# Moving work off the critical places of a transformer block on one TensorE: decays, modulation fillers, last head, residual loads

## The chip, the cores and the metric

The kernel runs on one core of a Trainium2 chip. A core has a matrix engine (TensorE, PE in the profile, with its weight loads as PEld), a vector engine (VectorE, DVE), a scalar engine (ScalarE, ACT), GpSimd (POOL), and queues that issue transfers (SyncE, SP). Each engine works through its own instructions in order and waits on semaphores for the others. The metric is the device time of one execution in microseconds; several runs are made and the median is given.

## What is computed

One layer of a generator over 512 latent tokens with 256 context tokens, width 2048, all in float32. The reference, cut to what matters here:

```python
mod = c_act @ w_mod + b_mod                       # six vectors of 2048: sh1, sc1, gt1, sh2, sc2, gt2
h  = rmsnorm(x, g_norm1) * (1 + sc1) + sh1        # and hc, the same for the context
z  = h @ w_in                                     # q, k, v, gates and decays of all heads
# 4 bidirectional GLA heads (gated linear attention), each decay a cumulative sum in the exponent
# 4 bidirectional mLSTM heads (matrix memory, running-max stabiliser)
y  = concat(rmsnorm(gla_o) * silu(gla_gate), sigmoid(ml_ogate) * rmsnorm(ml_h))
x  = x + gt1 * (y @ w_out)
h2 = rmsnorm(x, g_norm2) * (1 + sc2) + sh2
u_gate, u_val = split(h2 @ w_up)
x  = x + gt2 * ((silu(conv3x3(u_gate) + conv_b) * u_val) @ w_down)
out = rmsnorm(x, g_final)
```

`gt1`, `sh2`, `sc2` and `gt2` are four of the six modulation vectors. Each is a product of one vector with a 2048 x 2048 part of `w_mod`, so it costs much loading and little arithmetic. `gt1` is needed at the residual behind w_out, `sh2` and `sc2` for `h2`, `gt2` only at the residual behind w_down.

## The kernel before

All activations are held transposed: features on the 128 partitions, the 512 tokens along the free dimension. A product in float32 is made of three products (`mm3`): each operand is split into a high part, a rounded copy made by ScalarE, and a low part, the difference made by VectorE, and high x high, high x low and low x high are added up in PSUM. `load_split` brings one 512 KB piece of weights through SP's queue into a buffer of the pool `wraw` (four buffers), splits it into `hi` and `lo` (two buffers each), and hands both to the matmuls. A unit is eight such pieces (kp 0 to 7), each with 24 matmuls of 128x512 for four PSUM banks. So an engine that makes `hi` or `lo` late stops TensorE, and a `raw` buffer that is held too long delays the next load.

The stages, in order: the projection of heads 0 and 1; then for every further head its projection woven with the attention work of the head before (`weave`: a generator of stages says by its `yield`s how much projection, in estimated microseconds of TensorE, goes between two pieces of attention work). Heads 0 to 3 are GLA, heads 4 to 7 mLSTM. The last mLSTM head has no projection to be woven with and gets the first of four gate units. Then come gate units 1 to 3, the splitting of `yT`, four units of w_out with the residual `x2`, the second norm (`token_rstd`, `h2`), and the MLP: an `up_gate` unit, its 3x3 convolution on VectorE (eight multiply-adds per 128 features, `cv`), an `up_val` unit, and from time to time the blocks of w_down.

A GLA head works on levels. For each level `gla` makes a tile `ex`: two subtractions on VectorE, two exponentials on ScalarE, a multiplication with q and k, and then the matmuls `sl`. `ex` has two buffers. In the mLSTM head the blocks of tokens are called j; each makes `po`, a normaliser `dn` and the output `ob` on VectorE, and ends with `yield 1.4`.

The four late modulation vectors are made by fillers: small functions in a list. `load_split` pops `rate` of them per load (with a running `credit`). A chunk filler (`mod_chunk`) loads 512 KB of `w_mod` into a `wraw` buffer (`raw_m`); VectorE multiplies one half by a column and adds it up, ScalarE scales the other half, and POOL adds that up. The last of eight chunks adds the two sums on POOL (L259). An end filler (`mod_end`) makes four small matmuls (`mc`, L266), which are kept in program order among each other, and VectorE adds the bias (`mod`). Between chunks and end are entries that do nothing, as a lag. Regions 2, 3 and 4 make 132 entries, popped in the projections of heads 4 to 7 from kp 3 on, in the gate units and in w_out; region 5 makes 40, popped in the MLP behind 20 entries that do nothing.

A scheduler orders the instructions of each engine by priority and estimated readiness. TensorE's work keeps program order up to the end of the heads; work under `high_priority` goes first.

Of the kernel before, what the change touches and what calls it, by code (L numbers as in the profile page):

```python
# [26 lines left out]
H = 4  # L27
# [42 lines left out]
def block_kernel(ctx: ExitStack, tc: tile.TileContext, a: dict, out: bass.AP):  # L70
# [8 lines left out]
    def sub(o, x, y):  # L79
        V.tensor_tensor(out=o, in0=x, in1=y, op=ALU.subtract)  # L80
# [33 lines left out]
    csil = keep.tile([P, 128], F32, name="csil")[:, 0:KT]  # L114
    modc = {n: keep.tile([P, KT], F32, name=f"mod{n}") for n in (2, 3, 4, 5)}
    wraw = pool(ctx, "wraw", 4)
    whi = pool(ctx, "whi", 2)
    wlo = pool(ctx, "wlo", 2)
    actp = pool(ctx, "actp")
# [122 lines left out]
    def mod_chunk(region, n, kp, parts):  # L242

        name = f"m{region}_{n}_{kp}"
        raw = wraw.tile([P, 2, T], F32, name=f"raw_{name}", tag="raw")
        nc.sync.dma_start(raw, a["w_mod2"][region - 2, n, kp])
        if kp == 0:
            parts += [sum_tile(i, name) for i in range(2)]
        dv, po = parts
        ce, co = (csil[:, 2 * kp + i : 2 * kp + i + 1] for i in range(2))  # L250
        if kp == 0:
            V.tensor_scalar(out=dv, in0=raw[:, 0, :], scalar1=ce, scalar2=None, op0=ALU.mult)
            S.activation(po, raw[:, 1, :], AF.Copy, scale=co)
        else:
            V.scalar_tensor_tensor(out=dv, in0=raw[:, 0, :], scalar=ce, in1=dv, op0=ALU.mult, op1=ALU.add)  # L255
            S.activation(raw[:, 1, :], raw[:, 1, :], AF.Copy, scale=co)  # L256
            G.tensor_tensor(out=po, in0=po, in1=raw[:, 1, :], op=ALU.add)  # L257
        if kp == KP - 1:
            G.tensor_tensor(out=po, in0=po, in1=dv, op=ALU.add)  # L259
# [47 lines left out]
    def project_steps(h, banks):  # L307

        for kp in range(KP):
            rate[0] = 2 if h >= H and kp >= 3 else 0  # L310
            wh, wl = load_split(a["w_heads"][h, kp], f"h{h}_{kp}")
            for g in range(6):
                project_chunk(kp, wh, wl, banks[g], g)
                yield (1.36, 1.36, 1.44, 1.44, 1.04, 1.04)[g]
# [319 lines left out]
    def crossed(ex, b, fwd):  # L634
# [3 lines left out]
        at, step = (b, T - b) if fwd else (0, T + b)  # L638
        return bass.AP(ex.tensor, ex.offset + at, [ex.ap[0], [2 * b, n], [step, 2], [1, b]])

    def gla(h, pair, qk, v, kn, vn, yT, prep, fill, after, pending):
        bt, b2, kd, ends = (prep[n] for n in ("bt", "b2", "kd", "ends"))

# [8 lines left out]
                               op0=ALU.mult, op1=ALU.mult)  # L652
        yield fill
        for lv, b in enumerate(LEVELS + [P, 2 * P]):
            ex = wk2.tile([P, 2, T], F32, name=f"ex{h}_{lv}", tag="ex")
            n = T // (2 * b)
            if b < P:
                sf = bt[0].rearrange("p (n a b) -> p n a b", a=2, b=b)
                sb = bt[1].rearrange("p (n a b) -> p n a b", a=2, b=b)
                rf = sf[:, :, 0, b - 1 : b].unsqueeze(2).to_broadcast([P, n, 2, b])  # L660
                rb = sb[:, :, 1, 0:1].unsqueeze(2).to_broadcast([P, n, 2, b])
                sub(crossed(ex, b, True), sf[:, :, ::-1, :], rf)
                sub(crossed(ex, b, False), sb, rb)
                S.activation(ex[:, 0, :], ex[:, 0, :], AF.Exp, scale=DECAY)
                S.activation(ex[:, 1, :], ex[:, 1, :], AF.Exp, scale=-DECAY)
            else:
                for i in range(n):
                    e = 2 * i if b == P else 1
                    for s in range(2):
                        for d in range(2):  # L670

                            at = 2 * b * i + (b if s == d else 0)
                            S.activation(ex[:, s, at : at + b], b2[d][:, at : at + b], AF.Exp,
                                         scale=-DECAY if s else DECAY, bias=ends[:, s, d, e : e + 1])
            if pair:
                mul(ex, ex, pair[0])
            else:
                for i in range(2):
                    mul(ex[:, i, :], ex[:, i, :], qk[i])
            if b <= P:  # L680
                ps = psb(f"sl{h}_{lv}", (P, TJ, P))
                for i in range(TJ):
                    j = i if b < P else i ^ 1
                    mm(ps[:, i, :], ex[:, 1, P * i : P * i + P], ex[:, 0, P * j : P * j + P], start=True, stop=True)
                if b < P:
                    V.copy_predicated(scd, msk[:, lv, :].unsqueeze(1).to_broadcast([P, TJ, P]), ps)
                else:
                    S.copy(sc1, ps)
            else:
                for half in range(2):  # L690
                    ps = psb(f"sl{h}_{lv}_{half}", (P, 2, 2 * P))
                    for ii in range(2):
                        i = 2 * half + ii
                        j0 = 2 * P * (1 - half)
                        mm(ps[:, ii, :], ex[:, 1, P * i : P * i + P], ex[:, 0, j0 : j0 + 2 * P],
                           start=True, stop=True)
                    S.copy(sc2[half], ps)
            if lv == 0:
                pending()
            yield fill  # L700
            if lv in (2, 3, 4, 5, 6, 8):
                next(after, None)
            if lv == 1:

                for j in range(CJ):
                    mul(kd[:, :, j], kd[:, :, j], kn[j].unsqueeze(1).to_broadcast([P, 2, DK]))
                ps = psb(f"cst{h}", (P, 2, DV))
                for d in range(2):
                    for j in range(CJ):
                        mm(ps[:, d, :], kd[:, d, j, :], vn[j][:, 0:DV], start=(j == 0), stop=(j == CJ - 1))  # L710
                S.copy(s0[:, :, 0:DV], ps)
                qi = wtile(f"qi{h}", "qi", 2, T)
                for d in range(2):
                    S.activation(qi[:, d, :], b2[d], AF.Exp, scale=DECAY)
                mul(qi, qi, qk[0].unsqueeze(1).to_broadcast([P, 2, T]))
                yield 1
# [80 lines left out]
    def mlstm(h, _, qk, v, kn, vn, yT):  # L797
# [51 lines left out]
        for j in range(TJ):  # L849
# [16 lines left out]
                    V.scalar_tensor_tensor(out=ob[:, j, :], in0=po[:, 0:DV], scalar=dn, in1=ob[:, j, :],  # L866
                                           op0=ALU.mult, op1=ALU.add)
            S.activation(junk, ob[:, j, :], AF.Square, accum_out=ssq[:, j : j + 1])
            yield 1.4
        yield 5.6  # L870
        finish(h, ob, ssq, yT)

# [5 lines left out]
    def first_stages(tiles):  # L878

        yield from small_rows()  # L880
        prep = gla_prep(0, preps[0])
        for need in (0, 1.4, 0, 3, 1, 0):
            next(prep)
            yield need
        end = yield from gla(0, *tiles, yT, preps[0], 2.2, gla_prep(1, preps[1]), lambda: None)
        q, k, v0, v1, *c = early_sums
        tiles = ([], (q, k), [v[:, b, :] for v in (v0, v1) for b in range(2)],
                 [e[:, 0:DK] for e in c], [e[:, DK:] for e in c])
        end = yield from gla(1, *tiles, yT, preps[1], 2.2, gla_prep(2, preps[2]), end)
        yield 4  # L890
        end()

    def stages(h, tiles):

        yield 2.7
        if h >= H:
            yield from mlstm(h, *tiles, yT)
        elif h + 1 < H:
            end = yield from gla(h, *tiles, yT, preps[h], 4, gla_prep(h + 1, preps[h + 1]), lambda: None)
            yield 5  # L900
            end()
        else:
            end = yield from gla(h, *tiles, yT, preps[h], 2.6, iter(()), lambda: None)
            yield 5
            end()
            yield from ml_gates()

    tiles = evict(0, first)
    for h in range(1, 2 * H):
# [1 line left out]
            accs = [acc(f"a{h + 1}_{g}", BANKS[g]) for g in range(6)]  # L911
            steps = project_steps(h + 1, accs)
        else:
            rate[0] = 1.5
            accs = [acc(f"ga0_{i}") for i in range(4)]
            steps = unit_steps(a["w_gates"][0], "ga0", *hx, accs)
        weave(first_stages(tiles) if h == 1 else stages(h, tiles), steps)
# [9 lines left out]
    st_3 = ExitStack()  # L927
    gp = pool(st_3, "gp", 2)
    rp = pool(st_3, "rp")
    rate[0] = 1.5  # L930
    for g in range(4):
        if g:
            accs = unit(a["w_gates"][g], f"ga{g}", *hx)
        for i in range(4):
# [5 lines left out]

    tc.keep_in_program_order(S.preload_act_table_set("natural_log_exp_and_others"))

    yh, yl, x2 = [], [], []
    for k in range(KT):
        yh.append(acttile(k, "h", f"yTh{k}"))
        yl.append(acttile(k, "l", f"yTl{k}"))
        split(yh[k], yl[k], yT[k])
        x2.append(ytile(k, f"x2_{k}"))
        nc.sync.dma_start(x2[k], a["xT"][k])
    def residual(k, ps, gate, sl=slice(0, T)):  # L950
        xx = x2[k][:, sl]
        V.scalar_tensor_tensor(out=xx, in0=ps, scalar=gate[:, k : k + 1], in1=xx, op0=ALU.mult, op1=ALU.add)
# [28 lines left out]
    sums2 = []  # L981
    for n in range(4):
        accs = unit(a["w_out"][n], f"wo{n}", yh, yl)
        with tc.high_priority():
            for i in range(4):
                residual(4 * n + i, accs[i], modc[2])
# [18 lines left out]

    fp = pool(ctx, "fp")
    tp = pool(ctx, "tp", 4)
    cwt = fp.tile([P, NF, 9], F32, name="cwt")
    cbt = fp.tile([P, 152], F32, name="cbt")[:, 0:NF]
    nc.sync.dma_start(cwt, a["conv_w"])  # L1010
# [7 lines left out]
    def sum_tile(i, name):  # L1018
        return fp.tile([P, T], F32, name=f"sum{i}_{name}", tag=f"g{'hl'[i]}10")

    rate[0] = 1.5
    fillers += [lambda: None] * 20
    mod_fillers((5,), 2)

    def up_gate(q):
# [167 lines left out]
```

## Time and profile before

| | before |
|---|---|
| median of 3 runs | 2600.23 us (2597.21 to 2606.91) |
| profiled execution | 2597.59 us |
| its span | 2595.9 us |
| TensorE busy | 2541.1 us, 98% of the span |
| VectorE busy | 1356.0 us, 52% |
| mean granted TensorE clock | 0.994 |
| `raw_m` loads (modulation) | 192 of 512 KB, 4.4 us to landing |

The engines' rows give busy time, its share of the span and the number of instructions. In a list of waits, each row has the waiting engine, tile and line, then the engine, tile and line that released it, the total time, the number of times and the longest. In a timeline a row has the start, the duration, engine, line, operation and tiles, and in brackets the idle time before it with what ended that. In a row of windows the engines' busy times stand in the order PE, PEld, DVE, ACT, POOL (only POOL, or none, where one engine was asked for), then the granted clock of TensorE, the share of the DMA engines and GB/s.

### The profile page before, as it was taken

How to read it: one execution, taken by the hardware profiler on the slowest of the kernel's cores; microseconds unless marked ns; L12 is line 12 of the kernel's file. 1: busy time of each engine (PE TensorE's matmuls, PEld its weight loads, DVE VectorE, ACT ScalarE, POOL GpSimd, SP SyncE). 2: the span in 40 equal slices, each digit the busy share in tenths (PEclk: the TensorE clock that was granted, in tenths of full speed). 3: DMA queues.
4: the chain of work that ended last, by engine and by line, in shares of the span. 5: the costliest groups of instructions: out<-in, count | busy, mean ns of one | idle time of the engine just before them, and what ended most of it. 6: DMA issues, size and time to landing. Idle time of an engine off the chain costs nothing.

```text
span 2595.9 us, 31962 instructions
## 1 busy us (share of the span) xinstructions
PE 2541.1 (98%) x12882; PEld 2134.8 (82%) x12882; DVE 1356.0 (52%) x1969; ACT 873.9 (34%) x1289; POOL 228.1 (9%) x183
## 2 busy tenths in 40 slices
PE   6999999999999999999999999999999999999998
PEld 4887888888897888878878888888888888888887
DVE  6557765543334465458576336532653365336544
ACT  4225543332333343334433123312331233123332
POOL 0000001021222323210321000000000000000001
PEclk9999999999999999989999999999999999999999
DMA  9741112121333666532654222322232223222333
GB/s 383 269 155 34 33 41 90 66 98 66 122 122 126 214 226 216 199 114 101 211 178 141 96 97 97 98 97 98 98 98 98 97 98 97 96 96 87 100 97 102
DMA packets 96349, 321.39 MB, mean 124 GB/s; under 512 B 10884, under 2 KB 15304, under 8 KB 96200
## 3 DMA queue, kind: packets, MB, share of 16 engines
q1 hardware_dynamic: 96200, 319.34, 35.8%
q8 instruction: 101, 1.65, 0.3%
q14 instruction: 48, 0.39, 0.0%
HBM read 315.10 MB, written 4.19 MB: 123 GB/s over the span
## 4 chain that ended last, share of the span: by engine, by line
PE 89%; DVE 4%; DMA 4%; issue 1%; ACT 1%; POOL 1%; SPq 0%; POOLq 0%; ACTq 0%; DVEq 0%
PE a L95 18%; PE ug L95 18%; PE dn L95 17%; PE uv L95 17%; PE wo L95 6%; PE ga L95 5%; PE po L95 3%; DMA raw_m<-in_w_mod 2%; PE sl L95 1%; PE ps_m L95 1%; DVE cv L1040 1%; PE dl L95 1%; PE cst L95 0%; POOL sum_m L257 0%; PE s L95 0%
## 5 line engine op out<-in xcount | busy, mean ns | idle before, releaser
L95 PE MATMUL ug<-h2h,hi_ug 128*128 128x512 f32 x688 | 269.0, 392 | 1.6 <-ACT h2h L999 1.6
L95 PE MATMUL uv<-h2h,hi_uv 128*128 128x512 f32 x688 | 268.6, 390 | 1.5 <-ACT hi_uv L89 1.5
L95 PE MATMUL uv<-h2h,lo_uv 128*128 128x512 f32 x688 | 268.5, 390 | 1.4 <-DVE lo_uv L90 1.4
L95 PE MATMUL ug<-h2l,hi_ug 128*128 128x512 f32 x688 | 268.4, 390 | 0.0
L95 PE MATMUL ug<-h2h,lo_ug 128*128 128x512 f32 x688 | 268.4, 390 | 0.0
L95 PE MATMUL uv<-h2l,hi_uv 128*128 128x512 f32 x688 | 268.4, 390 | 0.0
L95 PE MATMUL dn<-gh,hi_d 128*128 128x512 f32 x644 | 250.5, 389 | 0.0
L95 PE MATMUL dn<-gl,hi_d 128*128 128x512 f32 x644 | 250.5, 389 | 0.0
L95 PE MATMUL dn<-gh,lo_d 128*128 128x512 f32 x644 | 250.5, 389 | 0.0
L1040 DVE SCALAR_TENSOR_TENSOR cv<-pad,cwt,cv 128x512 f32<-128x512 f32 x344 | 242.8, 765 | 10.6 <-ACT cv L1038 9.1
L90 DVE TENSOR_TENSOR lo_ug<-raw_ug,hi_ug 128x1024 fp32r<-128x1024 f32 (+1 forms) x88 | 107.3, 1220 | 240.0 <-ACT hi_ug L89 240.0
L257 POOL TENSOR_TENSOR sum_m<-sum_m,raw_m 128x512 f32<-128x512 f32 x112 | 175.6, 1568 | 576.2 <-ACT raw_m L256 335.7
L90 DVE TENSOR_TENSOR lo_uv<-raw_uv,hi_uv 128x1024 fp32r<-128x1024 f32 (+1 forms) x88 | 105.6, 1200 | 181.1 <-ACT hi_uv L89 180.6
L90 DVE TENSOR_TENSOR lo_d<-raw_d,hi_d 128x1024 fp32r<-128x1024 f32 x82 | 98.8, 1205 | 165.5 <-ACT hi_d L89 164.6
L89 ACT CAST hi_ug<-raw_ug 128x1024 fp32r<-128x1024 f32 (+1 forms) x88 | 90.9, 1033 | 266.6 <-PE ug L95 199.2
L89 ACT CAST hi_d<-raw_d 128x1024 fp32r<-128x1024 f32 x82 | 85.1, 1037 | 278.7 <-PE dn L95 224.4
L255 DVE SCALAR_TENSOR_TENSOR sum_m<-raw_m,csil,sum_m 128x512 f32<-128x512 f32 x112 | 97.9, 874 | 150.6 <-DMA raw_m<-in_w_mod 150.4
L89 ACT CAST hi_uv<-raw_uv 128x1024 fp32r<-128x1024 f32 (+1 forms) x88 | 90.9, 1033 | 251.0 <-PE uv L95 180.9
L95 PEld LDWEIGHTS uv<-h2h,lo_uv 128*128 128x128 f32 x688 | 129.6, 188 | 29.6 <-DVE lo_uv L90 2.7
L95 PEld LDWEIGHTS ug<-h2h,hi_ug 128*128 128x128 f32 x688 | 129.9, 189 | 28.9 <-ACT h2h L999 1.9
L95 PEld LDWEIGHTS uv<-h2h,hi_uv 128*128 128x128 f32 x688 | 129.4, 188 | 28.9 <-ACT hi_uv L89 2.0
L95 PEld LDWEIGHTS ug<-h2l,hi_ug 128*128 128x128 f32 x688 | 129.7, 189 | 27.0
(304 smaller groups left out, 5220.4 us busy)
## 6 DMA issues: line engine op xcount, KB each, us to landing
raw_m<-in_w_mod SPq DMA_DIRECT2D x192, 512.0 KB, 4.4
raw_ug<-in_w_up SPq DMA_DIRECT2D x80, 512.0 KB, 3.2
raw_uv<-in_w_up SPq DMA_DIRECT2D x80, 512.0 KB, 3.2
raw_d<-in_w_down SPq DMA_DIRECT2D x79, 512.0 KB, 3.3
raw_h<-in_w_heads SPq DMA_DIRECT2D x64, 512.0 KB, 3.2
raw_ga<-in_w_gates SPq DMA_DIRECT2D x32, 512.0 KB, 3.4
raw_wo<-in_w_out SPq DMA_DIRECT2D x32, 512.0 KB, 4.3
xl<-in_xT SPq DMA_DIRECT2D x16, 256.0 KB, 4.8
```

Source lines behind the costliest of these rows:

```text
L89: S.copy(hi, x)
L90: return V.tensor_tensor(out=lo, in0=x, in1=hi.bitcast(F32), op=ALU.subtract).ins
L95: ins = PE.matmul(*args, **kw)
L255: V.scalar_tensor_tensor(out=dv, in0=raw[:, 0, :], scalar=ce, in1=dv, op0=ALU.mult, op1=ALU.add)
L257: G.tensor_tensor(out=po, in0=po, in1=raw[:, 1, :], op=ALU.add)
L1040: V.scalar_tensor_tensor(out=t3, in0=src, scalar=w, in1=t3, op0=ALU.mult, op1=ALU.add)
```

## The change

1. The decays of the first two levels (subtractions and exponentials of `ex`) are put into `level_decays`, and `gla_ahead` calls it for levels 0 and 1 of a head before the projection of that head ends; `gla` then takes the two tiles from `prep`.
2. Fillers are popped at other rates: no longer in the projection of head 4 (`h > H` in place of `h >= H`), 1.75 in place of 1.5 per load in the gate units 0 to 2 and in w_out, 1 in gate unit 3, 1.25 in place of 1.5 in the MLP, where five idle entries stand ahead in place of 20.
3. Fillers load into own pools: `mraw3` (four buffers) from the gate units on, `mraw4` (three) in the MLP.
4. In the last head the `yield` after each block j is 3 in place of 1.4.
5. The 16 loads of `x2` are issued four per unit of w_out and not all at once.

```diff
     def mod_chunk(region, n, kp, parts):
-        raw = wraw.tile([P, 2, T], F32, name=f"raw_{name}", tag="raw")
+        raw = mod_raw[-1].tile([P, 2, T], F32, name=f"raw_{name}", tag="raw")
...
     def project_steps(h, banks):
-            rate[0] = 2 if h >= H and kp >= 3 else 0
+            rate[0] = 2 if h > H and kp >= 3 else 0
...
+    def level_decays(h, lv, bt):
+        b = LEVELS[lv]
+        n = T // (2 * b)
+        ex = wk2.tile([P, 2, T], F32, name=f"ex{h}_{lv}", tag="ex")
...
+        sub(crossed(ex, b, True), sf[:, :, ::-1, :], rf)
+        sub(crossed(ex, b, False), sb, rb)
+        S.activation(ex[:, 0, :], ex[:, 0, :], AF.Exp, scale=DECAY)
+        S.activation(ex[:, 1, :], ex[:, 1, :], AF.Exp, scale=-DECAY)
+        return ex
+
+    def gla_ahead(h, prep):
+        prep["ex"] = [level_decays(h, lv, prep["bt"]) for lv in range(2)]
...
-            yield 1.4
+            yield 1.4 if h < 2 * H - 1 else 3
...
+        gla_ahead(0, preps[0])
         end = yield from gla(0, *tiles, yT, preps[0], 2.2, gla_prep(1, preps[1]), lambda: None)
+        gla_ahead(1, preps[1])
...
         yield 4
         end()
+        gla_ahead(2, preps[2])
...
             yield 5
             end()
+            gla_ahead(h + 1, preps[h + 1])
...
-            rate[0] = 1.5
+            rate[0] = 1.75
             accs = [acc(f"ga0_{i}") for i in range(4)]
...
-    rate[0] = 1.5
+    mod_raw.append(pool(st_3, "mraw3", 4, waits="tile"))
+    rate[0] = 1.75
     for g in range(4):
+        if g == 3:
+            rate[0] = 1
...
+    rate[0] = 1.75
     yh, yl, x2 = [], [], []
     for k in range(KT):
...
-        x2.append(ytile(k, f"x2_{k}"))
-        nc.sync.dma_start(x2[k], a["xT"][k])
...
         accs = unit(a["w_out"][n], f"wo{n}", yh, yl)
+        for k in range(4 * n, 4 * n + 4):
+            x2.append(ytile(k, f"x2_{k}"))
+            nc.sync.dma_start(x2[k], a["xT"][k])
...
+    mod_raw.append(pool(ctx, "mraw4", 3))
...
-    rate[0] = 1.5
-    fillers += [lambda: None] * 20
+    rate[0] = 1.25
+    fillers += [lambda: None] * 5
     mod_fillers((5,), 2)
```

More of the change, by code (lines that the diff above doesn't have):

```diff
@@ L116, in block_kernel @@
     wraw = pool(ctx, "wraw", 4)
+    mod_raw = [wraw]
     whi = pool(ctx, "whi", 2)
@@ L639, in crossed @@
         return bass.AP(ex.tensor, ex.offset + at, [ex.ap[0], [2 * b, n], [step, 2], [1, b]])
+    def level_decays(h, lv, bt):
+        b = LEVELS[lv]
+        n = T // (2 * b)
+        ex = wk2.tile([P, 2, T], F32, name=f"ex{h}_{lv}", tag="ex")
+        sf = bt[0].rearrange("p (n a b) -> p n a b", a=2, b=b)
+        sb = bt[1].rearrange("p (n a b) -> p n a b", a=2, b=b)
+        rf = sf[:, :, 0, b - 1 : b].unsqueeze(2).to_broadcast([P, n, 2, b])
+        rb = sb[:, :, 1, 0:1].unsqueeze(2).to_broadcast([P, n, 2, b])
+        sub(crossed(ex, b, True), sf[:, :, ::-1, :], rf)
[5 more added lines that the diff above has]
+        prep["ex"] = [level_decays(h, lv, prep["bt"]) for lv in range(2)]
     def gla(h, pair, qk, v, kn, vn, yT, prep, fill, after, pending):
@@ L654, in gla @@
         for lv, b in enumerate(LEVELS + [P, 2 * P]):
-            ex = wk2.tile([P, 2, T], F32, name=f"ex{h}_{lv}", tag="ex")
-            n = T // (2 * b)
             if b < P:
[L658 to L665, printed above, removed]
-            else:
-                for i in range(n):
+                ex = prep["ex"][lv] if lv < 2 else level_decays(h, lv, bt)
+            else:
+                ex = wk2.tile([P, 2, T], F32, name=f"ex{h}_{lv}", tag="ex")
+                for i in range(T // (2 * b)):
                     e = 2 * i if b == P else 1
```

## The prediction

> **What bounds the kernel now.** I read the page first (busy shares, then the chain that ended last), then PE's table of waits, then PE's and VectorE's timelines where the waits lie, then a few windows for the granted clock.
>
> ```profile
> span 2595.9 us, 31962 instructions
> PE 2541.1 (98%) x12882; PEld 2134.8 (82%) x12882; DVE 1356.0 (52%) x1969; ACT 873.9 (34%) x1289; POOL 228.1 (9%) x183
> PE 89%; DVE 4%; DMA 4%; issue 1%; ACT 1%; POOL 1%; SPq 0%; POOLq 0%; ACTq 0%; DVEq 0%
> ```
>
> TensorE is busy 98% of the span and makes 89% of the chain. The change takes no matmul away, so only PE's idle time and the time in which its clock is low can be won. Where PE waits, by line and releaser (total, times, longest):
>
> ```profile
> PE ss_l L95 <- DVE sq_l L86: 18.6, 1, 18.6
> PE sl L95 <- DVE ex L83: 4.5, 5, 1.8
> PE uv L95 <- ACT hi_uv L89: 1.5, 1, 1.5
> PE uv L95 <- DVE lo_uv L90: 1.4, 3, 0.6
> PE ga L95 <- DVE lo_ga L90: 1.2, 1, 1.2
> PE po L95 <- DVE ed L83: 1.1, 1, 1.1
> PE wo L95 <- DVE lo_wo L90: 1.1, 2, 0.7
> ```
>
> The first, 18.6 us, is the start of the kernel and is not touched. The others are small and lie in four places that the change does touch. After two of them the clock is low as well:
>
> ```profile
> 450.00:455.00 5.00, 3.81 (x17) 3.21 (x15) 5.00 (x6) 2.65 (x5) 1.85 (x1) 0.70 0.31 107
> 1330.00:1340.00 10.00, 7.93 (x27) 5.79 (x26) 5.47 (x5) 4.27 (x5) 5.09 (x4) 0.83 0.86 288
> ```
>
> The number after POOL's is the granted clock. 0.70 over 5 us loses 5 x 0.30 = 1.5 us of matmul time, 0.83 over 10 us loses 1.7 us.
>
> **Part 1, decays ahead: 0.** The instruction orders of the two programs are the same on every engine, waits included, from the start to about 413 us of the profile, so through heads 0, 1 and 2. The scheduler had already put these subtractions and exponentials ahead; the new function only writes down that order. Nothing is hidden and nothing can be uncovered.
>
> **Part 2, no fillers in head 3's stage: +4.9 us** (gains are positive).
>
> ```profile
> 431.00 0.75 DVE L255 SCALAR_TENSOR_TENSOR sum_m<-raw_m,csil,sum_m 128x512 f32<-128x512 f32 x1 [3.69 <-DMA raw_m<-in_w_mod]
> 448.32 1.13 PE L95 MATMUL sl<-ex 128*128 128x128 f32 x8 [1.84 <-DVE ex L83]
> 455.37 1.13 PE L95 MATMUL sl<-ex 128*128 128x128 f32 x8 [1.57 <-DVE ex L83]
> ```
>
> With rate 2 only for h above 4, the projection of head 4 pops no filler. VectorE, in order, stood 3.69 us for one filler's transfer at 431.00; from then on it was late with `ex`, and PE waited 1.84 and 1.57 us. Both gaps and the low clock between them go: 1.84 + 1.57 + 1.5 = 4.9. VectorE gets back 3.69 us and 0.75 for each filler, more than either gap; what is late next is PE's own projection work. Bounds: 3.4 (clock dip stays) to 4.9.
>
> The ten pops that go from here are made up later: 30 + 14 + 28 + 8 + 56 = 136 after, 40 + 12 + 36 + 48 = 136 before, for 132 entries. The gate units keep 36; the last head takes 2 more, w_out 8 more.
>
> ```profile
> 1028.00:1150.00 122.00, 122.00 (x551) 101.22 (x550) 56.80 (x67) 41.43 (x51) 31.01 (x20) 1.00 0.54 182
> ```
>
> In most of w_out PE is never idle and VectorE is busy 56.8 of 122 us, so these pops cost 0 there; the cover is that half-empty VectorE. The last entry is popped after 52/1.75 = 29.7 of 32 loads against 44/1.5 = 29.3, still ahead of its use.
>
> **Part 3, last head, 3 instead of 1.4: +2.2 us.**
>
> ```profile
> 793.94 0.70 PE L95 MATMUL po<-c,qs 128*128 128x258 f32 x2 [1.14 <-DVE ed L83]
> 799.76 0.67 PE L95 MATMUL po<-c,qs 128*128 128x258 f32 x2 [0.69 <-DVE dn L859]
> 805.10 0.67 PE L95 MATMUL po<-c,qs 128*128 128x258 f32 x2 [0.24 <-DVE ob L866]
> 810.90 0.67 PE L95 MATMUL po<-c,qs 128*128 128x258 f32 x2 [0.70 <-DVE ob L866]
> 797.75 0.75 DVE L255 SCALAR_TENSOR_TENSOR sum_m<-raw_m,csil,sum_m 128x512 f32<-128x512 f32 x1 [3.35 <-DMA raw_m<-in_w_mod]
> 809.15 0.75 DVE L255 SCALAR_TENSOR_TENSOR sum_m<-raw_m,csil,sum_m 128x512 f32<-128x512 f32 x1 [2.24 <-DMA raw_m<-in_w_mod]
> ```
>
> The orders show that two steps of gate unit 0 (1.36 us each by the code's own estimate) stand between the blocks of `po` where one stood. The last three gaps, 0.69 + 0.24 + 0.70 = 1.6, are each shorter than one step and close. The first (1.14) lies before any of the new filling; it depends on which filler VectorE meets there, and I take half. 1.6 + 0.6 = 2.2; bounds 0 (the fillers, now 1.75 per load, stall VectorE again) to 2.8.
>
> **Part 4, own buffers in gates and w_out, 1.75 per load: +1.0 us.**
>
> ```profile
> 953.46 0.50 PE L95 MATMUL ga<-hTh,lo_ga 128*128 128x512 f32 x1 [1.20 <-DVE lo_ga L90]
> 987.97 0.50 PE L95 MATMUL wo<-yTh,lo_wo 128*128 128x512 f32 x1 [0.42 <-DVE lo_wo L90]
> 994.40 0.50 PE L95 MATMUL wo<-yTh,lo_wo 128*128 128x512 f32 x1 [0.66 <-DVE lo_wo L90]
> ```
>
> There are 2.3 us of gaps where unit 3 and the splits of `yT` meet. Weights no longer queue for buffers behind fillers, but more fillers stand ahead of each `lo` in VectorE's order (three ahead of the third load of a gate unit). Bounds -2 (three fillers of 0.75) to +2.3; 1.0 lies nearer the gap row, since the unit's rate falls to 1 there. x2 by blocks: 0; its transfers still go out a unit ahead of use, on SP behind w_out's weights, and a unit is over 40 us of matmuls.
>
> **Part 5, the MLP: +4.7 and -4.6 us.** The gain first:
>
> ```profile
> 1318.94 0.50 PE L95 MATMUL uv<-h2h,lo_uv 128*128 128x512 f32 x1 [0.32 <-DVE lo_uv L90]
> 1325.24 0.50 PE L95 MATMUL uv<-h2h,lo_uv 128*128 128x512 f32 x1 [0.56 <-DVE lo_uv L90]
> 1332.09 0.50 PE L95 MATMUL uv<-h2h,hi_uv 128*128 128x512 f32 x1 [1.54 <-ACT hi_uv L89]
> 1333.35 0.52 PE L95 MATMUL uv<-h2h,lo_uv 128*128 128x512 f32 x1 [0.53 <-DVE lo_uv L90]
> ```
>
> ```profile
> 1325.21 5.68 DMA raw_uv<-in_w_up
> ```
>
> The second table is a piece of the chain: `raw_uv` was issued late, because the buffers of the shared pool were held by fillers that VectorE had not reached through the convolutions. With own buffers that goes: 2.95 us of gaps and the 1.7 of clock, 4.7.
>
> The cost: with 5 no-ops in place of 20, the first chunks come in the first up_val unit, and the order puts the first four `mc` matmuls (L266) inside it, after two matmuls of its sixth load (kp 5). PE is in order there: everything behind waits for POOL's last addition.
>
> ```profile
> L95 PE MATMUL uv<-h2h,hi_uv x64: 389/389/389, 1207.3 to 1250.1; 128*128 128x512 f32 x64
> 1207.50:1251.00 43.50, 43.48 (x192) 1.00 0.40 145
> 1229.28 0.76 DVE L1040 SCALAR_TENSOR_TENSOR cv<-pad,cwt,cv 128x512 f32<-128x512 f32 x1
> 1229.94 0.76 DVE L255 SCALAR_TENSOR_TENSOR sum_m<-raw_m,csil,sum_m 128x512 f32<-128x512 f32 x1
> 1230.60 1.24 DVE L90 TENSOR_TENSOR lo_uv<-raw_uv,hi_uv 128x1024 fp32r<-128x1024 f32 x1
> 1231.74 2.59 DVE L1040 SCALAR_TENSOR_TENSOR cv<-pad,cwt,cv 128x512 f32<-128x512 f32 x2
> ```
>
> ```profile
> 1230.83 2.16 POOL L257 TENSOR_TENSOR sum_m<-sum_m,raw_m 128x512 f32<-128x512 f32 x1 [31.03 <-ACT raw_m L256]
> 1294.86 1.63 POOL L259 TENSOR_TENSOR sum_m<-sum_m,sum_m 128x512 f32<-128x512 f32 x1
> ```
>
> In before's times PE comes to that place at 1207.3 + 5 x 43.5/8 + 2 x 43.5/192 = 1234.9. VectorE's order there is `lo_uv` of kp 5 (ends 1231.84, and cannot come sooner: its buffer is freed by PE), then cv, sum, cv, sum at 0.66 apart: 1234.6. POOL's last addition, 1.63, ends at 1236.2: PE waits at least 1.2. While POOL added (2.16 at 1230.83), two cv took 2.59 instead of 1.42, so 0.54 of an addition's time is lost to VectorE; two additions of 1.57 (the mean of all on the page) before that place add 1.7. A stop of 2.9 us has the clock dip behind it like the two above, 1.7. Sum -4.6. Bounds: -1.2 (no contention, no dip) to -15.5 (all seven additions and the last one in full, 7 x 1.57 + 1.63 = 12.6, with 1.2 and 1.7). I take the value by the measured 0.54. SP's queue is also longer in front of `raw_uv`: the load of kp 4 stands behind a filler's that waits for an addition; it has several us of reserve, so 0.
>
> The Trainium skill, "SBUF — State Buffer", section "Who interferes with whom", says that a VectorE operation with two SBUF inputs and a GpSimd one that reads SBUF exclude each other for a whole instruction. By that, all additions would count in full if VectorE came second each time, which is the far bound; the row with 2.59 shows a little over half. "TensorE: Matmul & The Clock Gate", Part 1: The HAM clock gate, of the Trainium skill, has the half rate begin after an idle window of about 3.4 us; by that a stop of 2.9 us costs no clock and this part would be -2.9 in place of -4.6 (2590.3 in all). The rows differ: behind 1.84 and 1.54 us the clock was low, so I charge it.
>
> **Sum.** 4.9 + 2.2 + 1.0 + 4.7 - 4.6 = +8.2. The profiled execution took 2597.6 us (span 2595.9), 2.6 under the median of the three runs, 2600.2; so 2589.4 for it, and 2592.0 for the median.
>
> **Rivals.**
> All gaps close, nothing new: 4.9 + 2.8 + 2.3 + 4.7 = 14.7, 2585.5. For it: every named gap has its cause edited. Against it: the in-order `mc`, which is 1.2 us late even by the kindest rows. Chance 0.2.
> Slower, through VectorE and POOL in the first up_val unit: the additions block the convolutions in full, `lo_uv` and `mc` come late by 12.6 us and more, 15.5 with the dip, against 12.8 won: 2600.2 + 2.7 = 2603. It decides once PE loses more than 12.8 us in that unit. For it: VectorE has hardly a pause between 1205 and 1233. Against it: the fillers' first loads are there long before, so some additions come ahead of the convolutions. Chance 0.13, beyond 0.5% (which needs a further 10 us, from a second such unit) 0.06.
> The change does not do what it says: stalls only move with the fillers, as part 1 already changes no order; between 2597 and 2603. For it: VectorE waits for fillers' transfers all over the profile. Chance 0.17.
> My forecast, 2586 to 2597: 0.5.
>
> **Chances and range.** 0.5% is 13 us, about what a measurement of this kernel tells from none: faster means under 2587.2, slower over 2613.2. Faster comes from the first rival alone with the lower edge of the forecast, 0.22; slower 0.06; the rest 0.72. The range, 2580 to 2604, takes in the first rival below and most of the third and second above.
>
> **What would show it.** PE's wait for `ex` falls from 4.5 to about 1 and the clock near 450 stays full; no gap before `po` but the first; no waits for `hi_uv` and `lo_uv` in the second up_val unit; a new wait of 1 to 5 us of `mc` (or of the matmul behind it) on POOL near 1225 in the new time, perhaps with a low clock behind it. I am wrong if that wait is over 10 us, if it is nil, or if gaps of over 1 us come up before `lo_ga` or `lo_wo`.

## The result and the profile after

The changed kernel takes 2606.49 us (median of 12 runs, 2603.57 to 2609.52), the kernel before 2600.48 us in the same number of runs: 1.0024 of the time before, 95% interval 1.0016 to 1.0032. It is slower by about 6 us, where 8 us less were forecast; that is inside the 0.5% called "same", but outside the forecast's range and on the other side. The profiled execution took 2605.78 us.

The heading rows of the page after, and those of PE's waits after that lie where the change acts, by line and releaser (total, times, longest):

```profile
span 2603.9 us, 31925 instructions
PE 2543.7 (98%) x12882; PEld 2136.7 (82%) x12882; DVE 1373.8 (53%) x1969; ACT 870.8 (33%) x1289; POOL 225.7 (9%) x183
```

```profile
PE uv L95 <- DVE lo_uv L90: 4.0, 5, 1.4
PE mc L267 <- POOL sum_m L260: 3.1, 1, 3.1
PE mc L267 <- POOL ed L840: 2.5, 1, 2.5
PE ga L95 <- DVE lo_ga L90: 2.5, 3, 1.3
PE sl L95 <- DVE ex L83: 2.1, 3, 1.3
PE po L95 <- DVE ed L83: 2.1, 2, 1.2
PE po L95 <- ACT ob L876: 1.5, 2, 0.9
```

The waits for `ex` fell from 4.5 to 2.1, as the change meant. In their place stand two waits of `mc`, more waits for `lo_uv` and `lo_ga`, and waits of `po` on ScalarE, which the table before did not have. Where they lie, in PE's timeline:

```profile
452.84 1.13 PE L95 MATMUL sl<-ex 128*128 128x128 f32 x8 [1.31 <-DVE ex L83]
542.22 0.70 PE L95 MATMUL po<-c,qs 128*128 128x258 f32 x2 [0.84 <-DVE ed L83]
551.10 0.70 PE L95 MATMUL po<-c,qs 128*128 128x258 f32 x2 [0.58 <-ACT ob L876]
556.79 0.70 PE L95 MATMUL po<-c,qs 128*128 128x258 f32 x2 [0.95 <-ACT ob L876]
775.37 1.52 PE L267 MATMUL mc<-cst,sum_m 128*128 128x1 f32 x8 [2.54 <-POOL ed L840]
852.05 0.50 PE L95 MATMUL ga<-hTh,lo_ga 128*128 128x512 f32 x1 [1.26 <-DVE lo_ga L90]
1216.97 0.50 PE L95 MATMUL uv<-h2h,lo_uv 128*128 128x512 f32 x1 [0.76 <-DVE lo_uv L90]
1224.17 0.50 PE L95 MATMUL uv<-h2h,lo_uv 128*128 128x512 f32 x1 [1.44 <-DVE lo_uv L90]
1230.61 0.50 PE L95 MATMUL uv<-h2h,lo_uv 128*128 128x512 f32 x1 [0.69 <-DVE lo_uv L90]
1244.89 1.05 PE L267 MATMUL mc<-cst,sum_m 128*128 128x1 f32 x8 [3.11 <-POOL sum_m L260]
```

Two of them have low clock behind them (windows of the same trace; granted clock after POOL's number). 15 x 0.23 = 3.5 us and 10 x 0.17 = 1.7 us of matmul time are lost there:

```profile
770.00:785.00 15.00, 12.46 (x44) 9.39 (x43) 4.15 (x6) 6.88 (x13) 5.33 (x10) 0.77 0.51 172
1245.00:1255.00 10.00, 10.00 (x41) 8.26 (x42) 6.29 (x8) 4.46 (x6) 3.55 (x3) 0.83 0.79 274
```

So the losses are: 2.4 us in head 4, 2.5 + 3.5 behind the last head's `pg`, 2.5 in gate units 1 and 2 (three gaps, the longest shown), and 6.0 + 1.7 in the first up_val unit. The gains in head 3, the last head and the second up_val unit are real and smaller.

### The profile page after: what moved, and what is told of

Its sections match the earlier page's. It is cut to its first block, busy times and chain, and to the rows that moved or that the text cites. A ratio compares the mean times of both kernels' runs of the same rounds, so it can differ in the third digit from the quotient of the medians.

```text
span 2603.9 us, 31925 instructions
## 1 busy us (share of the span) xinstructions
PE 2543.7 (98%) x12882; PEld 2136.7 (82%) x12882; DVE 1373.8 (53%) x1969; ACT 870.8 (33%) x1289; POOL 225.7 (9%) x183
## 4 chain that ended last, share of the span: by engine, by line
PE 61%; DVE 3%; issue 2%; DMA 2%; ACT 1%; POOL 1%; POOLq 0%; SPq 0%; ACTq 0%; DVEq 0%
PE dn L95 17%; PE ug L95 16%; PE uv L95 15%; PE wo L95 7%; PE ga L95 4%; DVE cv L1063 2%; DMA raw_m<-in_w_mod 2%; PE dl L95 1%; DVE lo_uv L90 1%; PE po L95 0%; POOL sum_m L258 0%; DVE sum_m L256 0%; PE mc L267 0%; DVE lo_ga L90 0%; ACT raw_m L257 0%
## 5 line engine op out<-in xcount | busy, mean ns | idle before, releaser
L256 DVE SCALAR_TENSOR_TENSOR sum_m<-raw_m,csil,sum_m 128x512 f32<-128x512 f32 x112 | 110.3, 985 | 94.4 <-DMA raw_m<-in_w_mod 93.7
L95 PEld LDWEIGHTS uv<-h2l,hi_uv 128*128 128x128 f32 x688 | 129.6, 188 | 27.1
```

Source lines behind the costliest of these rows:

```text
L95: ins = PE.matmul(*args, **kw)
```

## The experiments

Two theories. A: the time is set by where fillers land; each loss is a filler's step on a place where an in-order engine has no reserve. B: each part keeps its own gain or loss wherever the fillers land, and what is lost comes from elsewhere (the own buffers' transfers, POOL, the clock). Ratios are to the kernel before on the same chip, with 95% intervals. The experiments ran on three chips, so times of different runs are compared by these ratios.

**Head 4's fillers put back.**

```diff
-            rate[0] = 2 if h > H and kp >= 3 else 0
+            rate[0] = 2 if h >= H and kp >= 3 else 0
```

> The changed kernel with the fillers put back into head 4's projection (which is woven with head 3). Theory A (each loss is a filler that lands on a place where an in-order engine has no reserve; taking fillers from head 3 pushed the following ones onto such places): the two gaps before sl in head 3 come back (about 3.4 us and 1.5 us of low clock), the three gaps before po in head 4 (2.4 us of waiting, 3.0 with what they cost around them) go, and the wait of mc behind pg at 772 us goes with its low clock (2.5 + 3.4 us): about 2602 to 2604. Theory B (head 3 without fillers is a gain of 4.9 and the losses come from elsewhere): about 2611.

Measured: 2598.69 us, 1.0001 (0.9991 to 1.0010), some 6 us under the changed kernel; what B expected is excluded. The gaps before `sl` are back, this time with no low clock:

```profile
447.61 1.13 PE L95 MATMUL sl<-ex 128*128 128x128 f32 x8 [1.70 <-DVE ex L83]
454.68 1.13 PE L95 MATMUL sl<-ex 128*128 128x128 f32 x8 [3.13 <-DVE ex L83]
```

And everything from head 4 to the end of w_out is free of waits. One window over this stretch, first of this run, then of the changed kernel:

```profile
490.00:1140.00 650.00, 649.89 (x3293) 552.80 (x3293) 317.68 (x498) 239.51 (x368) 152.71 (x120) 1.00 0.44 153
```

```profile
490.00:1140.00 650.00, 641.21 (x3231) 544.14 (x3231) 325.97 (x501) 240.93 (x374) 161.56 (x128) 0.99 0.47 158
```

PE is busy 649.89 of 650 us, against 641.21. So the gaps in head 4, behind `pg`, in the last head and in the gate units all came from one edit 100 to 450 us earlier: ten pops fewer put every later filler ten entries on. It came out better than A's 2602 to 2604; I had not counted the gaps of the gate units (2.5) and of the last head (1.2) to that edit. In head 4 the mechanism is the one seen in head 3 before: VectorE stands in order for fillers' transfers between the blocks of `po`. VectorE of the changed kernel:

```profile
549.21 0.75 DVE L256 SCALAR_TENSOR_TENSOR sum_m<-raw_m,csil,sum_m 128x512 f32<-128x512 f32 x1 [2.96 <-DMA raw_m<-in_w_mod]
554.90 0.75 DVE L256 SCALAR_TENSOR_TENSOR sum_m<-raw_m,csil,sum_m 128x512 f32<-128x512 f32 x1 [3.33 <-DMA raw_m<-in_w_mod]
```

**One idle entry ahead of the fillers.** `mc` moves away from `pg`, a load later.

```diff
+    fillers += [lambda: None] * 1
     mod_fillers((2, 3, 4), 3)
```

> The changed kernel with one idle entry ahead of all fillers of regions 2 to 4, so that every end comes one entry later; on TensorE the four mc that stood right behind the two pg of the last head move a load later. Theory A (mc takes the PSUM buffer of the first pg and must wait until ScalarE has read it, with the two buffers of that tag): the wait of 2.5 us is gone, and the half clock behind it (up to 3.4 us): 2601 to 2604. Theory B (POOL is the late one whatever stands in front): the wait moves with mc, 2606.

Measured: 2601.99 us, 1.0010 (1.0000 to 1.0019), as A expected. This `mc` did not wait any more (the one in the MLP still does, 3.07 us), and the gates' gaps went too; but head 4 got one gap of 4.03 us in place of three. One entry more or less moves the stalls. What `mc` waited for behind `pg` is narrowed by ScalarE's timeline of the changed kernel:

```profile
772.86 0.69 ACT L827 ACTIVATE qs<-pg,gccol 128x512 f32<-128x512 f32 x1 [0.23 <-PE pg L95]
773.45 1.78 ACT L837 ACTIVATE ed<-pg,acol 128x512 f32<-128x512 f32 x4
```

ScalarE's last reading of the first `pg` ends at 775.23, and `mc` starts at 775.37. Both share a tag with two buffers in PSUM, so `mc` needs the bank of the first `pg`. The profile names POOL's `ed`, which follows the same readings. In the kernel only ScalarE reads `pg`, and POOL's last addition for `mc` had ended at 750.75, so ScalarE is the likelier one; no run told the two apart.

**The MLP's old spread, own buffers kept.**

```diff
-    rate[0] = 1.25
-    fillers += [lambda: None] * 5
+    rate[0] = 1.5
+    fillers += [lambda: None] * 20
```

> The changed kernel with the MLP's old filler spread (20 idle entries, 1.5 per load), own buffers kept. Theory A (the early place in the first up_val unit costs 8.3 us: 3.2 before lo_uv, 3.1 before mc, the rest around them and in low clock): the first up_val unit has no gap, and the second has 1 to 3 us of gaps: 2597 to 2601. Theory B (the own buffers themselves cost, by transfers and SP's order): less than 2 us gained, 2605 or more.

Measured: 2601.47 us, 1.0011 (1.0002 to 1.0021), between what A and B expected. The wait of `mc` in the first up_val unit is gone, but not the three gaps before `lo_uv` (0.77, 1.46, 0.71 us, as in the changed kernel); the second unit has 2.6 us of gaps in place of 1.1. So A was wrong on their cause: the first sum stands on VectorE at 1198.44 us here and at 1200.18 in the changed kernel, though it is popped later here, and at 1228.88 before. With own buffers free, the scheduler puts the chunks' sums ahead of `lo_uv` and the convolutions at either spread.

**The MLP's fillers in the weights' buffers, early spread kept.**

```diff
-    mod_raw.append(pool(ctx, "mraw4", 3))
+    mod_raw.append(wraw)
```

> The changed kernel with the MLP's fillers back in the weights' buffers, early place and rate kept. Theory A (own buffers are a gain, the place is the loss): the gaps in the second up_val unit come back, 3 to 5 us, those of the first stay or grow: 2608 to 2613. Theory B (the own buffers make SP's queue wait and so cause the gaps of the first unit): 2600 to 2604.

Measured: 2610.52 us, 1.0043 (1.0028 to 1.0058). The time is A's, the reasons are not: the `lo_uv` gaps are gone, and instead PE waits twice for `mc`, once in each up_val unit, and once for `hi_uv`:

```profile
PE mc L267 <- POOL sum_m L260: 6.7, 2, 3.7
PE uv L95 <- ACT hi_uv L89: 1.8, 1, 1.8
```

The first sum stands at 1199.06 us here, so the early spread alone brings the sums forward as well. In time, own buffers are a gain with the early spread: 1.0024 against 1.0043.

**POOL's additions in the MLP thinned.** Region 5's additions on 16 of 512 columns; gt2 is then not what it should be.

```diff
-            G.tensor_tensor(out=po, in0=po, in1=raw[:, 1, :], op=ALU.add)
+            w = 16 if region == 5 else T
+            G.tensor_tensor(out=po[:, 0:w], in0=po[:, 0:w], in1=raw[:, 1, 0:w], op=ALU.add)
```

> The changed kernel with POOL's additions of region 5's chunks done on 16 of 512 columns only, so gt2 is not right; the loads, VectorE's and ScalarE's halves and every wait stay. Theory A (POOL's additions slow VectorE's convolutions and sums in the first up_val unit, 0.54 to 0.6 us for each us): cv is back at 0.67 us each there, the three gaps before lo_uv (2.9 us) mostly go, mc waits under 2 us: 4 to 7 us less than the changed kernel. Theory B (VectorE is late there because it waits for the fillers' transfers): the gaps stay, under 2 us gained.

Measured: 2602.07 us, 1.0011 (1.0001 to 1.0021), 3 to 4 us under the changed kernel by the ratios, just short of the 4 to 7 that A expected. VectorE in the first up_val unit, first of the changed kernel, then of this run:

```profile
1203.39 5.19 DVE L256 SCALAR_TENSOR_TENSOR sum_m<-raw_m,csil,sum_m 128x512 f32<-128x512 f32 x3
1210.96 4.82 DVE L1063 SCALAR_TENSOR_TENSOR cv<-pad,cwt,cv 128x512 f32<-128x512 f32 x4
1216.85 6.14 DVE L1063 SCALAR_TENSOR_TENSOR cv<-pad,cwt,cv 128x512 f32<-128x512 f32 x6
```

```profile
1204.86 1.53 DVE L256 SCALAR_TENSOR_TENSOR sum_m<-raw_m,csil,sum_m 128x512 f32<-128x512 f32 x2
1217.45 4.06 DVE L1064 SCALAR_TENSOR_TENSOR cv<-pad,cwt,cv 128x512 f32<-128x512 f32 x6
```

Six convolution steps take 6.14 us beside POOL and 4.06 with its additions thinned; three sums take 5.19 us beside POOL, two take 1.53 here. The 1.44 us gap is gone, and the gaps before `uv` in this unit fall from 2.9 to 1.6 us in all; those of the second unit, 1.1 us, are gone. `mc` still waits 3.31 us: its last sum stands in VectorE's order behind the convolutions, whatever POOL does.

**The MLP's fillers wholly as before**, once with head 4's fillers back and once without. Both edits are the two of the MLP above together (old spread, shared buffers).

> The changed kernel with the fillers of head 4's projection back and the MLP's fillers as before (the weights' buffers, 20 idle entries, 1.5 per load); what is left of the change is own buffers and 1.75 in gates and w_out, the 3 of the last head, and x2 by units. Theory A (these parts are a gain of 5 to 6 us by themselves: the gaps of 3.8 us before po and of 2.8 in the last gate unit and the first of w_out; the MLP's part is a loss of 4 to 5 us): no gap in the first up_val unit, those of before in the second: 2592 to 2595. Theory B (the MLP's part is no loss): 2598 or more.

> The changed kernel with only the MLP's fillers as before (the weights' buffers, 20 idle entries, 1.5 per load); head 4's projection stays without fillers. Theory A (the parts add up: the MLP's part costs 4 to 6 us, as between the two kernels with head 4's fillers back): a ratio to before of 1.000, the gaps in head 4, behind pg and in the gate units as in the changed kernel, none in the first up_val unit. Theory B (the MLP's own buffers were the gain, the loss lies before the MLP alone): 1.002 to 1.004.

Measured: 2593.03 us, 0.9978 (0.9969 to 0.9987) with head 4's fillers, 2602.64 us, 1.0003 (0.9989 to 1.0016) without. The MLP's part costs 0.0023 with and 0.0021 without (1.0001 to 0.9978, 1.0024 to 1.0003), some 5.5 us both times, and taking head 4's fillers away costs 0.0025 and 0.0023, some 6 us. Within intervals of 0.001 each way the two parts add up, and each is a loss as large as the whole; what remains of the change is a gain of 0.0022. How that gain is shared between the rates, the last head's 3 and the loads of `x2` was not tested.

With head 4's projection free of fillers, all four cases of the MLP were measured:

| spread | shared buffers | own buffers |
|---|---|---|
| old | 1.0003 | 1.0011 |
| early | 1.0043 | 1.0024 |

In the shared buffers the early spread is a clear loss, 0.0040. With own buffers it is 0.0013, at the edge of the noise. Own buffers with the old spread are not told from shared ones (0.0008), and with the early spread they took back 0.0019. So each change brings the sums forward, but own buffers by themselves are not shown to cost time.

**Own buffers in gates and w_out taken away as well.**

```diff
-    mod_raw.append(pool(st_3, "mraw3", 4, waits="tile"))
```

> The kernel with head 4's fillers back and the MLP as before, now also without the own buffers in gates and w_out; so rates 1.75, the last head's 3 and x2 by units alone. Theory A (it is the places of the fillers and not the buffers that closed the gaps in the last gate unit and the first of w_out): a ratio within 0.0005 of that with own buffers, 0.998. Theory B (the own buffers closed them): the gaps before lo_ga and lo_wo come back, 2 to 3 us: 0.999.

Measured: 2593.19 us, 0.9967 (0.9955 to 0.9979). This is 0.0011 under the run with own buffers, more than the 0.0005 of A but away from B, whose loss does not show: the time does not need the buffers. In the trace, gaps before `lo_wo` come back in part:

```profile
PE wo L95 <- DVE lo_wo L90: 1.8, 3, 0.8
```

The gaps before `lo_ga` do not, so these depend on the places, not the buffers. The intervals leave up to 2.6 us for the buffers.

**Decays alone**, on the kernel before.

```diff
+        gla_ahead(0, preps[0])
...
+                ex = prep["ex"][lv] if lv < 2 else level_decays(h, lv, bt)
```

> The kernel before with only the decays of levels 0 and 1 ahead. Every engine has the same instructions in the same order as before. Theory A (the scheduler had done this already): a ratio of 1.000, the gaps of before at the same places; what differs between the two traces is then only what differs from run to run, the place of the low clock above all. Theory B (the edit acts on something that the order does not show): more than 2 us either way.

Measured: 2601.73 us, 1.0009 (0.9998 to 1.0020). No engine's order differs, and no effect is shown. So the decays' move is not where the change loses or gains. The two profiled spans, 2595.9 and 2602.6, still differ by 6.7 us. Most of that is in one window, first before, then this run:

```profile
495.00:515.00 20.00, 20.00 (x130) 17.68 (x129) 16.03 (x20) 6.11 (x9) 0.00 (x0) 1.00 0.16 53
```

```profile
495.00:515.00 20.00, 20.00 (x78) 14.23 (x79) 11.80 (x14) 4.63 (x5) 0.00 (x0) 0.66 0.08 26
```

PE is never idle in either window; 20 x 0.34 = 6.8 us are lost to the granted clock.

**The last head's 3 alone**, on the kernel before.

```diff
-            yield 1.4
+            yield 1.4 if h < 2 * H - 1 else 3
```

> The kernel before with only 3 in place of 1.4 behind the blocks j of the last head. Theory A (two projection steps between the blocks cover the normaliser's chain): the gaps before the second to fourth po (0.69, 0.24, 0.70 us) go, the first (1.14) stays: 1.5 to 2.5 us faster. Theory B (VectorE stands for fillers' transfers that get longer with the spacing): gaps as before, no gain.

Measured: 2598.65 us, 1.000 (0.999 to 1.0009), no gain shown, though the interval leaves up to 2.6 us. The first gap stayed (1.13 us), three went, and one came, on ScalarE's `ob`, which itself came late because VectorE stood in order for a filler's transfer before the normaliser `dn`:

```profile
807.79 0.70 PE L95 MATMUL po<-c,qs 128*128 128x258 f32 x2 [1.36 <-ACT ob L864]
806.34 0.75 DVE L255 SCALAR_TENSOR_TENSOR sum_m<-raw_m,csil,sum_m 128x512 f32<-128x512 f32 x1 [3.95 <-DMA raw_m<-in_w_mod]
```

The gaps fell from 2.8 to 2.5 us. So A's cover works between the blocks, and B's stall takes most of it back.

**Fewer fillers in head 4's projection**, with the MLP as before: four (kp 6 and 7), or five (one per load from kp 3).

```diff
-            rate[0] = 2 if h > H and kp >= 3 else 0
+            rate[0] = 2 if h >= H and kp >= (3 if h > H else 6) else 0          # four
+            rate[0] = (2 if h > H else 1) if h >= H and kp >= 3 else 0          # five
```

> The kernel with the MLP as before, with four fillers in head 4's projection (kp 6 and 7) in place of ten, the rest of the change kept. Theory A (the gaps before sl in head 3 come from fillers popped from kp 3 on, while sl is due): those 5.7 us go, and what comes new is where the following fillers land; if they land well, 2587 to 2590, a ratio of 0.996. Theory B (the first unit of fillers stalls wherever it starts, as in head 4 in the changed kernel): gaps of 3 us or more in heads 3 or 4, 0.998 or more.

> As the run with four fillers, but with five, one per load from kp 3 on. Theory A (density decides): half of the 5.7 us of gaps before sl in head 3 goes, 0.997. Theory B (the first filler's transfer that VectorE must wait for decides, however many follow): the gaps stay, 0.998 or more.

Measured: four, 2593.54 us, 0.9969 (0.9959 to 0.9978); five, 2587.99 us, 0.9947 (0.9932 to 0.9962). With four, the gaps in head 3 fall to one of 1.3 us, and small ones come up in heads 5, 6 and the first gate units. With five, PE's waits are:

```profile
PE sl L95 <- DVE ex L83: 3.4, 3, 1.7
PE uv L95 <- DVE lo_uv L90: 1.8, 2, 1.3
PE cst L95 <- ACT ed L837: 1.1, 1, 1.1
```

One gap is left in head 3, and little after. The version with five, in four runs, is under both kernels, by 0.53% and 0.77%. The gaps in head 3 fell from 5.2 us with ten fillers to 1.5 with five, more than the half that A expected of density, and B's stall there did not come. Four and five differ by one entry, and most of the difference of their medians, 5.5 us, is not in the traces: the two profiled spans are 2587.5 and 2587.1 us, and PE's gaps differ by 1.3 us. The mean granted clock of the repeated runs was 0.9938 with four and 0.995 with five; on 2590 us that is an estimated 3 us. So it is not shown that five fillers are better than four.

## Why the prediction was wrong, by its own steps

**Decays ahead, 0:** right. The order showed it, and the run of this edit alone agrees within its interval.

**No fillers in head 3's stage, +4.9:** in place, the gain came: the gaps fell from 1.84 + 1.57 to 1.31 us and the 1.5 us of low clock went, 3.6 in all. The lower bound, in which the low clock stays as a cost of its own, misread the lines: it lies ahead of the second gap, and where it was absent that gap was longer by as much (3.13 in place of 1.57 us). The step that failed is the next: "the ten pops that go from here are made up later ... these pops cost 0 there; the cover is that half-empty VectorE". I looked only at the stage where the pops are finally made up. But a list popped in order moves as a whole: every filler came ten entries later up to the last head, and still eight at the end of the gate units. That put the first unit's transfers between head 4's `po` (2.4 us), the `mc` of one end filler behind the last head's `pg` (2.5 and 3.5 of clock) and later sums ahead of `lo_ga` in gate units 1 and 2 (2.5). I had costed the position of `mc` only in the MLP. In this the third rival (stalls only move with the fillers) was right, though the time came out above its 2597 to 2603.

**Last head, +2.2:** the place gained 1.6 (gaps of 2.8 to one of 1.2), but the run of this edit alone shows no gain in time, as the lower bound had it. What closes the gaps there is the fillers' place as much as the spacing: with head 4's fillers back, no gap is left there.

**Gates and w_out, +1.0:** measured -0.4 (gaps of 2.3 before, 2.7 after); the lower bound's mechanism, sums ahead of `lo`, was the one that came, made longer by POOL, and a gap of over 1 us before `lo_ga` was one of the prediction's own signs of being wrong. The places did it: with head 4's fillers back, at the same rates and buffers, no gap is left here either.

**The MLP, +4.7 and -4.6:** the second up_val unit gained 3.6 (the clock's 1.7, and gaps from 2.95 to 1.06). The cost was 7.7: 3.1 before `mc`, where 2.9 was taken, and 1.7 of clock as taken, but 2.9 before `lo_uv`, where the prediction had nothing. It counted two of POOL's additions; four sums stand ahead of the first `lo_uv`, and POOL made seven additions in the stretch from 1200 to 1222 us, where it made none before:

```profile
1200.00:1222.00 22.00, 22.00 (x98) 18.22 (x98) 18.18 (x25) 12.52 (x16) 0.00 (x0) 1.00 0.27 93
```

```profile
1200.00:1222.00 22.00, 21.24 (x94) 17.25 (x93) 21.76 (x19) 13.63 (x19) 14.11 (x11) 1.00 0.62 202
```

The first row is before, the second after; 2.4 of POOL's 14.1 us are other work. VectorE was idle for 3.8 us of this stretch before and for 0.2 after.

What one addition costs was read wrongly as well. The prediction set VectorE's loss, 1.17 us, against 2.16 us of POOL's time and took 0.54 of it. But POOL's time grows too when it comes second: that addition began 0.23 us behind `lo_uv`, and `lo_uv` was not slowed. With VectorE idle an addition takes 1.27 us, and a sum of 0.75 us takes 1.78 beside one:

```profile
1243.57 1.27 POOL L260 TENSOR_TENSOR sum_m<-sum_m,sum_m 128x512 f32<-128x512 f32 x1 [23.79 <-DVE sum_m L256]
840.96 1.78 DVE L256 SCALAR_TENSOR_TENSOR sum_m<-raw_m,csil,sum_m 128x512 f32<-128x512 f32 x1
```

The operation that came second was held up for 1.03 us there, and six convolution steps beside two additions by 6.14 - 4.06 = 2.08, 1.04 for each. Seven additions make 7.3 us, where the prediction's sum had 1.7. By the same measure the three sums lost 3.1 and four convolution steps 2.1 us, so all seven were paid in full. The Trainium skill, "SBUF — State Buffer", section "Who interferes with whom", says that a VectorE instruction with two SBUF inputs contends with a GpSimd instruction that reads SBUF, and that the shared ports are an exclusive lock. The trace agrees: the loss is nearly a whole addition each time, 1.04 of 1.27 us.

So the mechanism of the second rival (the slower one: additions block in full) came, at half its price, 7.7 in place of 15.5, because VectorE's idle time took up part of it, and the first rival (nothing new) did not.

The sum by the trace: +3.6 - 2.4 - 6.0 + 1.6 - 0.4 - 7.7 + 3.6 = -7.7, and the spans differ by 8.0. Of the rest, the granted clock was low for 3.4 us longer near 212 us and for 3.4 us less at the second norm; that these cancel is chance.

## What to carry to other kernels

A list of background work that is popped in order cannot be thinned at one place: everything behind it moves, so look in the new order at every place where it now meets an in-order engine without reserve, and not only where it is taken away or added. Before popping background work earlier or giving it its own buffers, ask what held it back so far; here late pops and the wait for a shared buffer together kept it out of VectorE's busiest stretch, and either one changed brought it in. Test the parts one by one: two parts of this change were a loss of about 6 us each, the rest a gain of about 6. And where engines share a port, count every operation on the other side, at what it costs alone.

## What the runs showed of the hardware

The granted clock differs between runs of the same order. Two programs with the same order on every engine had a low stretch of 13.6 us (6.8 us lost) in one profile at a place where the other had none. Both had PE busy there, but the place is not just any: of the fourteen profiles, four have a low stretch here, and each begins 2.8 to 3.0 us behind the start of the same small matmuls, `pre`, on 16 x 4 of the array, ahead of which PE is idle for 0.34 us:

```profile
493.87 1.02 PE L95 MATMUL pre<-glr,cst 16*4 16x512 f32 x4 [0.34 <-ACT yT L575]
497.00:510.00 13.00, 13.00 (x44) 8.47 (x43) 5.64 (x9) 2.77 (x4) 0.00 (x0) 0.50 0.12 40
```

These two rows are of the run with the decays alone. Whether `pre` is the cause was not tested. Gaps of 3.11 and 3.13 us in head 3 had no low clock behind them in two runs (head 4's fillers back, with the MLP as before and as changed), the same gap of 3.13 us had in three others, and one of 1.84 us had in the kernel before. This is as large as the effect studied, so a single profile of either kernel says little; the verdicts here rest on the repeated runs. The Trainium skill, "TensorE: Matmul & The Clock Gate", Part 1: The HAM clock gate, tells of a free-running window of 3.4 us that makes the clock differ from run to run; the dips of some 3.4 us here (449.6 to 453.0 us in the profile before) agree with that, but an idle gap shorter than the window, 1.84 us, was enough for one.
